# Sixty-six products of zeros in eleven moving-row forms, set between the two products of the first SwiGLU

## The chip, the cores and the metric

The kernel runs on one core of one Trainium2 chip. The metric is device time in microseconds (us), the median over runs of the whole program; lower is better. Profile times are counted from the start of the span, which runs from the first to the last instruction.

## The reference

One layer of a streaming encoder on an input of 1024 tokens by 1024 channels, in float32. The part that matters here is the first of three residual sub-layers:

```python
def swiglu_ffn(x, w_in, w_out):
    gate, up = jnp.split(x @ w_in, 2, axis=-1)
    return (jax.nn.silu(gate) * up) @ w_out

h = h + 0.5 * swiglu_ffn(rmsnorm(h, norm_ffn1[l]), ffn1_w_in[l], ffn1_w_out[l])
# w_in: 1024 x 5632, w_out: 2816 x 1024
# then: one projection to q, k, v, gates and pool; retention; pooling; merge; output product
# then: a second SwiGLU of the same shape, and a last RMSNorm
```

## The kernel before, in words

Every large product is done with one level of Strassen's scheme or more: the operands are cut into blocks (L11 to L22 for the weights, R11 to R22 for the activations), sums of blocks (S1 to S4, T1 to T4) are made on VectorE, and seven products of blocks take the place of eight. Each operand is held as two float32r tiles, a rounded part and the rest, and a product of two operands is three TensorE products (`mm3`, lines 181, 182 and 183): rounded by rounded, rounded by rest, rest by rounded. ScalarE writes the rounded part (line 161, `copy(hi, src)`) and VectorE the rest (line 162, `tt(lo, src, hi, SUB)`). One TensorE product has 128 by 128 weights and mostly 512 moving columns; in the steps made by `common` it has 256. Each has a weight load of its own.

The program is one stream of steps. A step is a pair: `prep`, which issues the loads, the block sums and the splits, and `body`, which issues TensorE's products and the work on their results. `Flow.run` issues the prep of a step four steps (`LOOK`) ahead of its body, and after every body some small items from a queue of follow-up work. A scheduler then orders the instructions of each engine by this order and by when their buffers come free, so an engine may run well ahead of the order of the text where its inputs and buffers are there. Each engine then works through its own list in order; DMAs are nearly all issued by SyncE (SP), also in order.

The buffers are rings. The ones that the change uses are `raw` (4 tiles of 128 by 1024 float32, which receive weights from memory), `c2` (8 tiles of 128 by 512 float32, which hold block sums and half results) and `ps` (6 banks of PSUM, taken with `bank`). The split weights of a step go to a ring of 5 tiles, `wt`.

The first SwiGLU, `ffn1`, runs two generators one after the other. `ffn_in` makes the gate and up halves, 22 groups of 128 channels each, the last two of them as a pair from `pairs_of_both` and `common`; its tiles carry the prefix `a`. Its last steps in TensorE's order are the products into `a_x`, `a_b` and `a_e`. `ffn_out` makes the second product, 11 blocks of the inner dimension, with tiles of the prefix `b`: first the alternating steps `p1` and `p6` for all 11 blocks (`bp1a`, `bp6b` in PSUM), then `p2` and `p7`, and so on. `p1` and `p6` take their weights from `bra` and `bL22a` and block sums `bs` (lines 886 to 888); `bL22a` is a `raw` tile for two blocks at a time, and from block 4 on `bra` is one too. The activations (`br`) are read back from the memory to which `ffn_in` wrote them.

At the start of the kernel, before any weight has arrived, twelve products of bfloat16 zeros (`set<-zero`, line 204) already run on TensorE.

Of the kernel before, what the change touches and what calls it, by code (L numbers as in the profile page):

```python
# [11 lines left out]
F32R = mybir.dt.float32r  # L12
BF16 = mybir.dt.bfloat16
AF = mybir.ActivationFunctionType
ALU = mybir.AluOpType
ADD, SUB, MUL = ALU.add, ALU.subtract, ALU.mult

P = 128
S = 1024
D = 1024  # L20
KT = D // P
H = S // 2  # L22
# [28 lines left out]
N_MV, N_T4, N_RAW, N_WT, N_TL, N_C2 = 28, 9, 4, 5, 4, 8  # L51
# [39 lines left out]
def block_kernel(ctx: ExitStack, tc, x, x_tok, vecs, f1_in, f1_out, w_in, w_v, pool_w, w_ret, w_pool, w_o,  # L91
                 f2_in, f2_out, g_row, rope, decay, consts, out, out_tok):
    nc = tc.nc
    mm = nc.tensor.matmul
# [3 lines left out]
    copy = nc.scalar.copy  # L98
# [4 lines left out]
    sb = ctx.enter_context(tc.tile_pool(name="sb", bufs=1))  # L103
# [16 lines left out]
    def raw(name):  # L120
        return sb.tile([P, S], F32, tag="raw", bufs=N_RAW, name=name)
# [7 lines left out]
    def c2(name):  # L129
        return sb.tile([P, H], F32, tag="c2", bufs=N_C2, name=name)  # L130

    def bank(name):
        return ps.tile([P, H], F32, tag="ps", name=name)

    def sum_bank(name):

        return ps.tile([P, H], F32, tag="sum", bufs=N_SUM, name=name)
# [8 lines left out]
    def spill(name, n, width=S):  # L146
        return [dr.tile([P, width], F32, tag=f"{name}{i}", name=f"{name}{i}") for i in range(n)]

    def half(t, j):
        return t[:, j * H : (j + 1) * H]  # L150
# [49 lines left out]
    for n in range(N_SUM):  # L200
        b = sum_bank(f"set{n}")
# [913 lines left out]
    gates = spill("gt", 2 * KT)  # L1115
    pm, ret = spill("pm", KT), spill("ret", KT)

    def ffn1():
        for n, step in enumerate(ffn_in(first, f1_in, ops1, "a", lead)):
            flow.rate = 1  # L1120
            yield step
        flow.rate = 2
        yield from ffn_out(first, ops1, ops_done["a"], f1_out, x, "b", mix.quarter, end1)

    mix = Next("n2", V_MIX, h1)
# [795 lines left out]
    def second():  # L1921
        for n, step in enumerate(ffn_in(ffn2, f2_in, ops2, "c")):
            flow.rate = 1
            yield step
        flow.rate = 2
    flow.run(chain(ffn1(), projections(), retention(), merge(), second(),
                   ffn_out(ffn2, ops2, ops_done.setdefault("c", set()), f2_out, h2, "d", fin.quarter, fin.end, fin)))
    flow.some(-1)
# [86 lines left out]
```

## Time and profile before

| | before |
|---|---|
| runs, us | 2138.69 and 2139.97, median 2139.33 |
| span of the profiled execution, us | 2137.8 |
| time of the profiled execution | not listed apart; the runs lie 0.9 to 2.2 us above the span |
| TensorE (PE) busy | 2127.8 us, 10798 products |
| weight loads (PEld) busy | 1808.3 us, 10798 loads |
| VectorE (DVE) busy | 1873.2 us, 3352 instructions |
| ScalarE (ACT) busy | 1100.9 us, 2082 instructions |
| GpSimd (POOL) busy | 0.2 us, 4 instructions |
| mean granted TensorE clock | 0.999 |

A product's busy time is longer than its share of the time, since products are pipelined: one with 512 columns is shown as 389 ns, but the next starts before it has ended. What one product costs is therefore read from the number of products in a stretch. In a table by stretches each engine has its busy time and, in brackets, the number of its instructions that touch the stretch.

### The profile page before, as it was taken

To read this page: it belongs to the slowest core of one execution; us is meant where nothing else is said; L and a number is where in the kernel's file an instruction comes from. 1 tells how busy PE (TensorE), PEld (TensorE's weight loads), DVE (VectorE), ACT (ScalarE), POOL (GpSimd) and SP (SyncE) were. 2 spreads that over 40 slices of the span, in tenths; PEclk is the share of its full clock that TensorE was granted. 3 is DMA by queue.
4 is the path that set the end of the run, shared out by engine and by line. 5 is a ranking of instruction groups with operands and counts; after the bars stand their busy time and mean duration, and the time that the engine had idled before them with its cause. 6 is when DMAs were issued, how large, how long until landed. Compare 5 with 4: busy or idle time off the path is not lost.

```text
span 2137.8 us, 30138 instructions
## 1 busy us (share of the span) xinstructions
PE 2127.8 (100%) x10798; PEld 1808.3 (85%) x10798; DVE 1873.2 (88%) x3352; ACT 1100.9 (51%) x2082; POOL 0.2 (0%) x4
## 2 busy tenths in 40 slices
PE   9999999999999999999999999999999999999998
PEld 7888888888888888888888998888888888888887
DVE  8798888997986799999988988899988988899796
ACT  8544444454654534454457753456644544455454
POOL 0000000000000000000000000000000000000000
PEclk9999999999999999999999999999999999999999
DMA  7232323675543333332336666624133232358542
GB/s 251 83 133 75 138 84 129 202 266 187 172 138 98 110 109 119 109 124 104 119 129 223 197 226 236 236 89 163 64 103 119 87 126 85 132 199 276 192 138 99
DMA packets 116391, 313.60 MB, mean 147 GB/s; under 512 B 12817, under 2 KB 17041, under 8 KB 116241
## 3 DMA queue, kind: packets, MB, share of 16 engines
q1 hardware_dynamic: 115664, 310.63, 42.7%
q8 instruction: 84, 1.38, 0.3%
q10 hardware_dynamic: 576, 1.05, 0.1%
q14 instruction: 67, 0.54, 0.1%
HBM read 220.93 MB, written 90.70 MB: 146 GB/s over the span
## 4 chain that ended last, share of the span: by engine, by line
PE 94%; DVE 4%; ACT 1%; DMA 1%; issue 0%; SPq 0%; ACTq 0%; DVEq 0%
PE c_b L181 2%; PE c_b L182 2%; PE c_b L183 2%; PE a_b L181 2%; PE a_b L182 2%; PE a_b L183 2%; PE c_e L182 2%; PE c_e L181 2%; PE c_e L183 2%; PE a_e L182 2%; PE a_e L181 2%; PE a_e L183 2%; PE a_a L181 1%; PE a_a L183 1%; PE a_a L182 1%; PE c_a L181 1%
## 5 line engine op out<-in xcount | busy, mean ns | idle before, releaser
L182 PE MATMUL c_b<-n3T,c_wS 128*128 128x512 f32 x176 | 68.6, 390 | 0.0
L183 PE MATMUL c_b<-n3T,c_wS 128*128 128x512 f32 x176 | 68.5, 389 | 0.0
L181 PE MATMUL c_b<-n3T,c_wS 128*128 128x512 f32 x176 | 68.4, 390 | 0.0
L182 PE MATMUL a_b<-n1T,a_wS 128*128 128x512 f32 x168 | 65.4, 389 | 0.0
L181 PE MATMUL a_b<-n1T,a_wS 128*128 128x512 f32 x168 | 65.4, 389 | 0.0
L183 PE MATMUL a_b<-n1T,a_wS 128*128 128x512 f32 x168 | 65.3, 389 | 0.0
L181 PE MATMUL a_a<-n1R,a_wL 128*128 128x512 f32 x120 | 46.7, 389 | 0.0
L182 PE MATMUL a_a<-n1R,a_wL 128*128 128x512 f32 x120 | 46.7, 389 | 0.0
L183 PE MATMUL a_a<-n1R,a_wL 128*128 128x512 f32 x120 | 46.7, 389 | 0.0
L182 PE MATMUL c_a<-n3R,c_wL 128*128 128x512 f32 x112 | 43.6, 389 | 0.0
L181 PE MATMUL c_a<-n3R,c_wL 128*128 128x512 f32 x112 | 43.6, 389 | 0.0
L183 PE MATMUL c_a<-n3R,c_wL 128*128 128x512 f32 x112 | 43.6, 389 | 0.0
L183 PEld LDWEIGHTS c_b<-n3T,c_wS 128*128 128x128 f32 x176 | 33.0, 188 | 6.9
L182 PEld LDWEIGHTS c_b<-n3T,c_wS 128*128 128x128 f32 x176 | 33.0, 188 | 6.8 <-DVE n3T L162 0.2
L181 PEld LDWEIGHTS c_b<-n3T,c_wS 128*128 128x128 f32 x176 | 33.0, 188 | 6.8 <-ACT n3T L161 0.3
L183 PEld LDWEIGHTS a_b<-n1T,a_wS 128*128 128x128 f32 x168 | 31.5, 188 | 6.6
L181 PEld LDWEIGHTS a_b<-n1T,a_wS 128*128 128x128 f32 x168 | 31.5, 188 | 6.5
L182 PEld LDWEIGHTS a_b<-n1T,a_wS 128*128 128x128 f32 x168 | 31.5, 188 | 6.3
L162 DVE TENSOR_TENSOR a_wS<-a_S,a_wS 128x512 fp32r<-128x512 f32 x45 | 31.0, 690 | 6.7 <-ACT a_wS L161 6.7
L161 ACT CAST c_wS<-c_S 128x512 fp32r<-128x512 f32 x46 | 27.9, 624 | 13.2 <-DVE c_S L455 7.1
L182 PE MATMUL c_e<-n3T,c_wL 128*128 128x512 f32 x88 | 34.5, 393 | 0.0
L181 PE MATMUL c_e<-n3T,c_wS 128*128 128x512 f32 x88 | 34.4, 391 | 0.0
(3385 smaller groups left out, 8156.9 us busy)
## 6 DMA issues: line engine op xcount, KB each, us to landing
c_ra<-in_f_in SPq DMA_DIRECT2D x22, 512.0 KB, 3.8
c_rb<-in_f_in SPq DMA_DIRECT2D x22, 512.0 KB, 3.7
a_ra<-in_f_in SPq DMA_DIRECT2D x21, 512.0 KB, 3.9
a_rb<-in_f_in SPq DMA_DIRECT2D x21, 512.0 KB, 3.9
t<-au SPq DMA_DIRECT2D x11, 512.0 KB, 2.8
b<-ag SPq DMA_DIRECT2D x11, 512.0 KB, 4.3
r<-au SPq DMA_DIRECT2D x11, 512.0 KB, 3.7
bra<-in_f_out SPq DMA_DIRECT2D x11, 512.0 KB, 6.3
```

What stands on the lines that cost most here:

```text
L161: copy(hi, src)
L162: tt(lo, src, hi.bitcast(F32), SUB)
L181: mm(dst, w[0], m[0], start=start, stop=False, skip_group_check=True)
L182: mm(dst, w[0], m[1], start=False, stop=False, skip_group_check=True)
L183: mm(dst, w[1], m[0], start=False, stop=stop, skip_group_check=True)
```

## The change

A new step, made by `forms`, is put between the last step of `ffn_in` and the first of `ffn_out`. Its prep takes two `raw` tiles (`fz`, `fm`) and three `c2` tiles (`fh`, `fy`, `fv`), sets them to zero on VectorE, copies `fz` to `fm` as float32r on ScalarE, does three multiplications by 1 and three copies of 128 by 512 on VectorE, and four subtractions of 128 by 512 on GpSimd, which read `fz` and `fy` and write the second half of `fz`. Its body issues eleven kinds of product, six of each, into one PSUM bank that nobody reads. The weights are 128 columns of `fm` (float32r) or of `fh` (bfloat16); the moving rows are 512 elements of the same tiles, taken in these forms:

| form | rows |
|---|---|
| `m[:, :H]`, `m[:, 8 : H + 8]` | 512 neighbours, from element 0 and from element 8 |
| `h[:, :H]`, `h[:, H:]` | 512 neighbours, bfloat16 |
| `two` | two runs of 256, 512 apart |
| `lines` | 32 runs of 16, 32 apart |
| `pairs_` | every second element |
| `turns` | runs of 16, in turn from the first and the second half of the tile |
| `apart` | single elements, in turn from the first and the second half of the tile |
| `same` | the same 16 elements 32 times |
| `one` | the same element 512 times |

```diff
     gates = spill("gt", 2 * KT)
     pm, ret = spill("pm", KT), spill("ret", KT)
 
+    def forms():
+
+        t = {}
+
+        def prep():
+            z = raw("fz")
+            nc.vector.memset(z, 0.0)
+            t["m"] = sb.tile([P, S], F32R, tag="raw", bufs=N_RAW, name="fm")
+            copy(t["m"], z)
+            t["h"] = sb.tile([P, 2 * H], BF16, tag="c2", bufs=N_C2, name="fh")
+            nc.vector.memset(t["h"], 0.0)
+            y, v = c2("fy"), c2("fv")
+            nc.vector.memset(y, 0.0)
+            for n in range(3):
+                nc.vector.tensor_scalar(v, y, 1.0, None, MUL)
+            for n in range(3):
+                nc.vector.tensor_copy(v.bitcast(F32R), y)
+            for n in range(4):
+                nc.gpsimd.tensor_tensor(half(z, 1), half(z, 0), y, SUB)
+
+        def body():
+            m, h = t["m"], t["h"]
+            w = m[:, S - P :]
+            lines = m.rearrange("p (a b c) -> p a b c", b=2, c=16)[:, :, 0]
+            pairs_ = m.rearrange("p (a b) -> p a b", b=2)[:, :, 0]
+            two = m.rearrange("p (a b c) -> p a b c", a=2, b=2)[:, :, 0]
+            turns = m.rearrange("p (b a c) -> p a b c", b=2, c=16)[:, :16]
+            apart = m.rearrange("p (b a) -> p a b", b=2)[:, :256]
+            same = m[:, :16].unsqueeze(1).to_broadcast([P, 32, 16])
+            one = m[:, :1].to_broadcast([P, H])
+            kinds = [(w, m[:, :H]), (h[:, :P], h[:, :H]), (w, two), (w, lines), (w, pairs_), (w, turns), (w, apart),
+                     (w, same), (w, one), (h[:, :P], h[:, H:]), (w, m[:, 8 : H + 8])]
+            b = bank("forms")
+            for l, r in kinds:
+                for n in range(6):
+                    mm(b, l, r, start=n == 0, stop=n == 5)
+
+        return prep, body
+
     def ffn1():
         for n, step in enumerate(ffn_in(first, f1_in, ops1, "a", lead)):
             flow.rate = 1
             yield step
         flow.rate = 2
+        yield forms()
         yield from ffn_out(first, ops1, ops_done["a"], f1_out, x, "b", mix.quarter, end1)
```

## The prediction

> **What bounds the kernel now.** I read the busy times first, then TensorE's waits, then a table by stretches.
>
> ```profile
> span 2137.8 us, 30138 instructions
> PE 2127.8 (100%) x10798; PEld 1808.3 (85%) x10798; DVE 1873.2 (88%) x3352; ACT 1100.9 (51%) x2082; POOL 0.2 (0%) x4
> PE 94%; DVE 4%; ACT 1%; DMA 1%; issue 0%; SPq 0%; ACTq 0%; DVEq 0%
> ```
> ```profile
> engine line waited for: us in total, times, longest us
> PE set L204 <- DVE zero L199: 1.2, 1, 1.2
> PE a L181 <- ACT n1R L165: 0.8, 2, 0.6
> PE a L182 <- DVE n1R L166: 0.6, 2, 0.3
> PE wo0e L183 <- DVE wo0wS L162: 0.4, 1, 0.4
> PE px L181 <- DVE g3A L1158: 0.4, 1, 0.4
> PE st L182 <- DVE v L162: 0.2, 1, 0.2
> ```
>
> TensorE is busy for all but 10.0 of 2137.8 us and carries 94% of the chain that ended last. Its listed waits are small, and none of them is at the place of the change: those on `set`, `a` and `n1R` are in the kernel's first steps, `px`, `st` and `wo0e` belong to the pooling, retention and merge, after the first SwiGLU. So TensorE is a conveyor: what is put on it makes the kernel longer by its full length, and there is no idle stretch near the place into which it could fall. What remains is to price a product in each form, and to ask whether the preparation delays TensorE or relieves it.
>
> ```profile
> core 0: us, PE busy (x) PEld busy (x) DVE busy (x) ACT busy (x) POOL busy (x), PEclk, DMA share, GB/s
> 408.00:414.00 6.00, 6.00 (x34) 5.22 (x33) 5.93 (x11) 3.90 (x8) 0.00 (x0) 1.00 0.96 300
> 414.00:423.00 9.00, 9.00 (x56) 8.01 (x55) 7.53 (x13) 4.51 (x8) 0.00 (x0) 1.00 0.99 362
> 423.00:440.00 17.00, 17.00 (x76) 14.08 (x75) 17.00 (x28) 6.63 (x12) 0.00 (x0) 1.00 0.52 194
> 430.00:630.00 200.00, 200.00 (x884) 165.58 (x884) 171.06 (x281) 104.68 (x185) 0.00 (x0) 1.00 0.60 199
> ```
> ```profile
> 422.58 0.39 PE L183 MATMUL a_e<-n1T,a_wL 128*128 128x512 f32 x1
> 422.81 0.39 PE L181 MATMUL bp1a<-bp1m,bp1w 128*128 128x512 f32 x1
> ```
>
> The second fence is TensorE's timeline at the seam: the last product of the first half starts at 422.58, the first of the second half at 422.81, with nothing between. The change goes there. The first fence shows TensorE full on both sides of it, and VectorE nearly so: idle for 0.07 us in 408 to 414, 1.47 in 414 to 423 and not at all in 423 to 440.
>
> **The price of one product.** The stretch from 430 to 630 holds only 512-column products of float32 tiles. 884 of them touch it; one that started up to 0.39 us before also counts, so each costs (200 + 0.39) / 884 = 0.2267 us, its weight load hidden (PEld counts 884 too). The bfloat16 price comes from the end of the kernel's opening products:
>
> ```profile
> 5.41 0.38 PE L204 MATMUL set<-zero 128*128 128x512 bf16 x1
> 5.63 0.38 PE L204 MATMUL set<-zero 128*128 128x512 bf16 x1
> ```
>
> These start 0.22 us apart: one spacing only, but it says that bfloat16 rows, of half the bytes, are hardly cheaper. Nine of the eleven kinds are float32r, 54 products of 0.2267 = 12.24 us; two are bfloat16, 12 of 0.22 = 2.64 us. At the plain price the body is 14.88 us.
>
> **The price of the form.** The trace has nearly no moving rows that are not neighbours. The nearest is the scores' product of line 1558, which takes two runs of 128 from the two halves of an operand tile:
>
> ```profile
> 1153.54 0.28 PE L182 MATMUL g2b<-n2R,g2ws 128*128 128x256 f32 x1
> 1153.66 0.28 PE L182 MATMUL s<-q,k 128*128 128x256 f32 x1
> 1153.77 0.28 PE L1558 MATMUL s<-q,k 128*128 128x256 f32 x1
> 1153.89 0.44 PE L181 MATMUL g3e<-n2T,g3wL 128*128 128x512 f32 x1
> ```
>
> It takes 0.12 us to the next start, as its plain neighbours do (0.12 and 0.11): one jump inside a row costs at most the 0.01 us that the view resolves. `two` has one jump, `lines` and `turns` have 31, `same` returns 31 times, `one` never moves, and the row from element 8 only starts elsewhere. For these I take the plain price. Below it they can't go far: bfloat16 rows, with half the bytes to fetch, save only 0.007 each, so even if `same` and `one` saved that, it is 0.1 in all. Upwards the bound is 0.01 per jump, 0.31 for a product of `lines` or `turns`.
>
> `apart` jumps at every element, 511 times, and `pairs_` skips every second one. The lower end is nothing extra. The upper end, 0.01 per jump, is 5.1 us for one product of `apart`, 30.7 for its six. I take twice the plain price for `apart`, one further element's time (0.44 ns) per jump: a jump of that size would be invisible in the row of line 1558, which is the nearest, and a jump at every element leaves no neighbour to share a fetch with. That adds 6 x 0.2267 = 1.36 us. `pairs_` I leave at the plain price; twice would add another 1.36.
>
> The Trainium skill, "Advanced Engine Details and Errata", section "SBUF Cachelines", says that SBUF is read in lines of 16 bytes and that at least two hits on a line are needed for full speed. By it only `apart` would pay (each of its elements leaves the line that the one before it was on) and `pairs_`, with two elements on each line, would not; it gives no amount, and no row here shows such a pattern.
>
> So the body is 14.88 + 1.36 = 16.24 us on TensorE, all of it on the path.
>
> **The preparation.** These rows give its prices:
>
> ```profile
> L199 DVE MEMSET zero<- x1: 272/272/272, 0.9 to 0.9; 128x256 uint32 x1
> L1658 DVE TENSOR_SCALAR o<-o,ir0r x8: 343/347/348, 1207.0 to 1209.2; 128x256 f32<-128x256 f32 x8
> L162 DVE TENSOR_TENSOR a_wS<-a_S,a_wS 128x512 fp32r<-128x512 f32 x45 | 31.0, 690 | 6.7 <-ACT a_wS L161 6.7
> L763 ACT ACTIVATE ag<-ag 128x1024 f32<-128x1024 f32 x22 | 23.4, 1062 | 11.7 <-DVE ag L755 7.3 <-DVE ag L758 4.3
> ```
>
> VectorE: the zeros are 1024, 512 and 512 words, 8 times the 256 words that took 0.272, so at most 2.2 us. The three multiplications of 512 lie between the 0.35 of 256 columns and twice that, the three copies (no row) between the same 0.35 and the 0.69 of a 512-column instruction with two inputs: together 2.1 to 4.2. VectorE gets 4.3 to 6.4 us of new work. ScalarE gets one copy, about 1.06 us, on an engine half idle here (4.51 of 9.00). GpSimd's four subtractions have no row; VectorE's form of the same instruction is 0.69, so at least 2.8 us for four; with GpSimd otherwise empty they cost nothing by themselves. Above, I allow 16 us, the body's length, beyond which they would outlast the cover.
>
> Does this hold TensorE up ahead of the body? What is queued behind the new instructions on VectorE are the last evacuations and the last split of the first half:
>
> ```profile
> 417.28 0.42 DVE L589 TENSOR_TENSOR ag<-a_x,ag 128x256 f32<-128x256 f32 x1
> 417.62 0.68 DVE L162 TENSOR_TENSOR a_wL<-a_rb,a_wL 128x512 fp32r<-128x512 f32 x1
> ```
> ```profile
> 419.38 0.28 PE L181 MATMUL a_x<-n1R22y,a_ws 128*128 128x256 f32 x1
> 420.53 0.39 PE L183 MATMUL a_e<-n1T,a_wL 128*128 128x512 f32 x1
> ```
>
> The product into `a_x` at 419.38 must wait until the addition that ends at 417.70 has read the bank: 1.7 us of slack. The first product with the rest part of `a_wL` starts at 420.53, 2.2 us after its split ends at 418.30. Before them VectorE is not doing only urgent work. It makes block sums for the second half far ahead:
>
> ```profile
> L886 DVE TENSOR_TENSOR bs<-bra,bL22a x11: 686/694/704, 405.0 to 463.0; 128x512 f32<-128x512 f32 x11
> L140 SPq DMA_DIRECT2D bL22a<-in_f_out x11: 327/371/994, 398.1 to 458.3; - x11
> ```
>
> The first of these sums is made at 405.0, for a step `p6` that starts twelve products after 422.81, at 425.5. This run-ahead work gives way to the new work, and the body's 16 us then repay it: VectorE gains 16 us and owes 4.3 to 6.4, plus what GpSimd takes from it. So most of the preparation is hidden. If it fell whole ahead of the two rows above, TensorE would stop for 6.4 - 1.7 = 4.7 us; at best for 0. I take 0.8, about one VectorE instruction that comes at the wrong moment, nearer to 0 because there are some 12 us of VectorE's list between 405.0 and 417.3 in which sums can be exchanged for zeros.
>
> The rings. `fz` and `fm` take two of four `raw` tiles, so `bL22a`, first loaded at 398.1, comes later, and `fm` is held until the body ends, near 439. The next claims of those two tiles are the loads of block 4, first needed by the step eight steps (8 x 12 x 0.2267 = 21.8 us) after the body; SP may stand at one of them until 439, with the later loads queued behind it, and 20 us are left for a landing and a split. The first `bL22a`, moved to some 412 to 418, is needed at 425.5 + 16 = 441. The three `c2` tiles and the bank come after tiles whose readers are done or stand on TensorE itself. I cost the rings at nothing; without the body's cover the late `bL22a` would cost TensorE several us.
>
> **Sum.** 16.24 + 0.8 = 17.0 us. The span becomes 2154.8; the median lies 1.5 above the span, so the time becomes 2156.3. That is 0.8% more, within the 2% (42.8 us, that is 2182.1) that a measurement of this kernel can surely tell from no change.
>
> **Rivals.**
>
> 1. GpSimd holds VectorE up. Both engines read the same tiles, and no row shows GpSimd at work beside VectorE. If each subtraction, at 1.4 us (twice VectorE's 0.69), kept VectorE out for its length, VectorE would lose 5.6 us besides the 4.3 to 6.4, just in 408 to 423, where it has 1.5 us to spare: TensorE stops for up to 5.6 + 6.4 - 1.7 = 10 us, likelier about 5: 2161, at most 2166. For it: VectorE's full rows; against it: the run-ahead work. The Trainium skill, "SBUF — State Buffer", section "Who interferes with whom", speaks for this: a VectorE instruction with two SBUF inputs contends with a GpSimd instruction that reads SBUF, and the later one is blocked until the first is done. No run here shows it yet. Chance 0.17.
>
> 2. Rows apart are dear (the slower side). If a jump costs close to what the view can hide, 9.1 ns, `apart` takes 0.23 + 511 x 0.0091 = 4.9 us a product instead of 0.45: 2156.3 + 6 x 4.45 = 2183, over 2%. It decides from about 9 ns a jump, some twenty times the time of one element. For it: nothing excludes it; against it: the row of line 1558. At 1 to 5 ns a jump it adds 0.5 to 2.6 us to a product: 2158 to 2170. Chance 0.12 for the milder form, 0.03 over 2%.
>
> 3. The body costs less than its count: the 16 us of cover for VectorE take away waits of TensorE later, or the products overlap something. Against it: only 10 us of idle TensorE exist, and most of that in the opening. At most 4 us: 2145 to 2152. Chance 0.08.
>
> 4. The products aren't there in the end (nobody reads their bank), and only the preparation is left: 2139 to 2142. Nothing in the trace speaks for it; the opening products, whose banks nobody reads either, are there in the profile. Chance 0.02.
>
> The forecast itself, 2152 to 2160, has 0.58. The range, 2150 to 2168, takes in rival 1, most of the milder rival 2 and part of rival 3, and leaves out the rest. Faster by over 2% needs 42.8 us that TensorE doesn't lose anywhere: 0.01. Slower by over 2%: 0.03 and 0.01 for a stall that I haven't seen. Within: 0.95.
>
> **What the changed profile would show.** 66 more products (10864) and as many loads; a stretch of some 16 us between the last `a_e` and the first `bp1a` in which only they run, at 0.227 for the float32 kinds, 0.22 for bfloat16, 0.45 for `apart`. TensorE's idle time should grow by less than 1 us. Wrong would be: gaps ahead of the body with VectorE or GpSimd as their releaser (rival 1), other forms over 0.3 or `apart` over 1 us (rival 2), a gap after the body that waits for `bL22a` or `bra` (the rings).

## The result, and the profile after

| | before | after |
|---|---|---|
| runs, us | 2138.69 and 2139.97, median 2139.33 | 2156.92 and 2157.77, median 2157.35 |
| span of the profiled execution, us | 2137.8 | 2154.8 |

The ratio is 1.0085, with a 95% interval of 1.0056 to 1.0115: 18.0 us more, within 2%. Forecast were 2156.3 and a span of 2154.8. The totals fit well; the terms behind them do not, as the profile shows.

First the page's totals and TensorE's list of waits (in total, times, longest):

```profile
span 2154.8 us, 30287 instructions
PE 2145.1 (100%) x10862; PEld 1819.8 (84%) x10864; DVE 1881.4 (87%) x3361; ACT 1102.9 (51%) x2083; POOL 5.8 (0%) x8
```
```profile
PE set L204 <- DVE zero L199: 1.2, 1, 1.2
PE g2b L181 <- ACT g2ws L161: 0.5, 1, 0.5
PE wo0e L183 <- DVE wo0wS L162: 0.4, 1, 0.4
PE a_x L181 <- DVE ag L589: 0.3, 1, 0.3
```

Idle TensorE is 9.7 us against 10.0 before: the whole growth of the span, 17.0 us, is busy time. (Two product records are missing from this trace, so it counts 10862 and not 10864.) One wait is new at the place of the change, that of `a_x` for the addition of line 589, one of the two that the prediction had named. By the starts of the products on both sides TensorE lost 0.49 us there.

TensorE's timeline, the first recorded product of each kind in the order of the code, and the first product of the next step. The columns are start, duration, engine and line:

```profile
422.36 0.39 PE L1153 MATMUL forms<-fm 128*128 128x512 f32 x1
423.95 0.38 PE L1153 MATMUL forms<-fh 128*128 128x512 bf16 x1
424.84 0.58 PE L1153 MATMUL forms<-fm 128*128 128x512 f32 x1
426.42 0.41 PE L1153 MATMUL forms<-fm 128*128 128x512 f32 x1
427.90 0.61 PE L1153 MATMUL forms<-fm 128*128 128x512 f32 x1
430.60 0.42 PE L1153 MATMUL forms<-fm 128*128 128x512 f32 x1
432.06 0.38 PE L1153 MATMUL forms<-fm 128*128 128x512 f32 x1
433.35 0.39 PE L1153 MATMUL forms<-fm 128*128 128x512 f32 x1
434.78 0.38 PE L1153 MATMUL forms<-fm 128*128 128x512 f32 x1
436.09 0.39 PE L1153 MATMUL forms<-fh 128*128 128x512 bf16 x1
438.79 0.40 PE L181 MATMUL bp1a<-bp1m,bp1w 128*128 128x512 f32 x1
```

The body takes 438.79 - 422.36 = 16.43 us; 16.24 was forecast. A kind's price is the difference of two starts, divided by six. The fifth kind, `pairs_`, takes (430.60 - 427.90) / 6 = 0.450 us a product, and the seventh, `apart`, (433.35 - 432.06) / 6 = 0.215. The prediction had it the other way round: 0.2267 and 0.4534. `lines` takes 0.247, `turns` 0.243, `same` 0.238, `one` 0.218.

What the preparation did is in the timeline of VectorE and GpSimd (the lists of `fz` and `fv`: duration minimum, median and maximum in ns, then first and last start):

```profile
L1136 POOL TENSOR_TENSOR fz<-fz,fy x4: 1294/1360/1620, 409.0 to 413.5; 128x512 f32<-128x512 f32 x4
```
```profile
L1132 DVE TENSOR_SCALAR fv<-fy x3: 1402/1402/1515, 410.8 to 413.8; 128x512 f32<-128x512 f32 x3
L1134 DVE CAST fv<-fy x3: 414/420/426, 416.0 to 417.4; 128x512 fp32r<-128x512 f32 x3
```
```profile
408.00:414.00 6.00, 6.00 (x39) 5.38 (x39) 5.69 (x7) 2.01 (x5) 4.76 (x4) 1.00 0.41 128
440.00:460.00 20.00, 20.00 (x90) 16.56 (x89) 17.80 (x29) 9.34 (x16) 0.00 (x0) 1.00 0.85 273
```
The second of these stretches in the kernel before:
```profile
440.00:460.00 20.00, 20.00 (x90) 16.54 (x89) 20.00 (x35) 11.87 (x21) 0.00 (x0) 1.00 0.88 302
```

Each subtraction on GpSimd takes 1.36 us, and beside them the three multiplications on VectorE take 1.4 us each, as long as a subtraction, while the copies of the same size after them take 0.42. The third fence is the table by stretches (columns as in the prediction): between 408 and 414 VectorE gets through 7 instructions where it got through 11 before. Yet by 440 to 460 it has idle time, 2.2 of 20 us, where before it had none: the body's 16 us gave back more than the preparation took.

### The profile page after: what moved, and what is told of

Read it like the earlier page. It is cut to its first block, busy times and chain, and to the rows that moved or that the text cites. A ratio compares the mean times of both kernels' runs of the same rounds, so it can differ in the third digit from the quotient of the medians.

```text
span 2154.8 us, 30287 instructions
## 1 busy us (share of the span) xinstructions
PE 2145.1 (100%) x10862; PEld 1819.8 (84%) x10864; DVE 1881.4 (87%) x3361; ACT 1102.9 (51%) x2083; POOL 5.8 (0%) x8
## 4 chain that ended last, share of the span: by engine, by line
PE 93%; DVE 5%; DMA 1%; issue 1%; ACT 1%; SPq 0%; ACTq 0%; DVEq 0%
PE c_b L181 2%; PE c_b L182 2%; PE c_b L183 2%; PE a_b L181 2%; PE a_b L183 2%; PE a_b L182 2%; PE c_e L182 2%; PE c_e L181 2%; PE c_e L183 2%; PE a_e L181 2%; PE a_e L182 2%; PE a_e L183 2%; PE a_a L181 1%; PE a_a L183 1%; PE a_a L182 1%; PE bp6b L183 1%
```

## Experiments

Ratios are against the kernel before on the same chip, whose median there was 2138.64 to 2138.77 us.

### All products of one kind

```diff
-            kinds = [(w, m[:, :H]), (h[:, :P], h[:, :H]), (w, two), ...
+            kinds = [(w, apart)] * 11      # apart66
+            kinds = [(w, pairs_)] * 11     # step2_66
```

> All 66 products take single elements in turn from two halves of the tile. As the prediction priced it (0.4534 each) the body is 29.9 us and the time 2139.3 + 29.9 + 0.8 = 2170.0; as the trace after shows it (0.216) the body is 14.3 us and the time 2139.3 + 14.3 + 0.5 = 2154.1.

> All 66 products take every second element. As the prediction priced it (0.2267 each) the time is 2139.3 + 15.0 + 0.8 = 2155.1; as the trace after shows it (0.452) the body is 29.8 us and the time 2139.3 + 29.8 + 0.5 = 2169.6. With the run of single elements in turn this is the reverse of the prediction's two choices, whose errors would cancel in the sum.

Measured: `apart66` 2155.21 us (ratio 1.0079, 1.0062 to 1.0096), `step2_66` 2171.34 (1.0150, 1.0135 to 1.0165). The two differ by 16.1 us, 0.244 a product; the prices in the trace after differ by 0.235. In the traces of these two kernels the 66 products take 14.24 us (421.81 to 436.05) and 29.90 us (421.87 to 451.77), that is 0.216 and 0.453 each. So the prediction's two choices were each wrong, in opposite directions, and nearly equal in size. In the whole change, with six products of each, the errors cancelled by luck.

### Which rows are dear

Two kernels with other rows in the step of zeros, eight products of each kind, without the multiplications, copies and subtractions. They are read by the starts of the products alone; each ran once (2159.49 and 2164.39 us). These functions make the rows, and the rest of the edit is left out:

```diff
+            def alt(x, n=2):
+                return x.rearrange("p (b a) -> p a b", b=n)
+            def near(x, n):
+                return x.rearrange("p (c b a) -> p c a b", b=2, a=n)
+            def step(n):
+                return m.rearrange("p (a b) -> p a b", b=n)[:, :, 0]
+            def runs(n):
+                return m.rearrange("p (a b c) -> p a b c", b=2, c=n)[:, :, 0]
+            def swap(n):
+                return m.rearrange("p (b a c) -> p a b c", b=2, c=n)[:, : H // (2 * n)]
```

> The step of zeros with other rows: thirteen kinds, eight products each, no GpSimd and no VectorE work beyond setting the zeros. It is read by the spacing of the products. Theory A, of the trace after: float32 rows come from one stretch of memory at about 9.0 bytes per ns (512 neighbours, 2048 bytes, 0.227 us; every second element, 4096 bytes of stretch, 0.452), and two places far apart supply twice that, so that TensorE's own 0.216 is left. It expects 256 columns of every fourth element 0.45 and 128 columns of every eighth 0.45 (0.23 if a fetch is 16 bytes or less), and 0.216 for the distances 512 and 256; at which smaller distance the gain ends is open. Theory B, of the prediction: every jump costs, so distances 512, 256, 128, 64 all take 0.45, and every fourth or eighth element costs the plain price of its width, 0.113 and about 0.11. Theory C: the 11 ns between 0.227 and 0.216 come from the weights, read from the same tile as the rows; then neighbours with weights from another tile take 0.216.

The first table's timeline, first products: `near(q, 4)` (order 0, 4, 1, 5, 2, 6, 3, 7 in every eight elements), four runs in turn, 256 columns of every fourth element, 128 of every eighth:

```profile
433.98 0.38 PE L1151 MATMUL forms<-fm 128*128 128x512 f32 x1
435.70 0.43 PE L1151 MATMUL forms<-fm 128*128 128x512 f32 x1
439.79 0.39 PE L1151 MATMUL forms<-fm 128*128 128x256 f32 x1
441.64 0.40 PE L1151 MATMUL forms<-fm 128*128 128x128 f32 x2
```

At a distance of 16 bytes a product takes (435.70 - 433.98) / 8 = 0.215 us; the distances 64, 256, 512, 1024 and 2048 bytes took 0.216 too, four runs 0.283. 256 columns of every fourth element take (441.64 - 439.79) / 8 = 0.231, and not 0.45, so what counts is not the stretch of memory spanned; 256 neighbours take half of it, 0.12. 128 columns of every eighth element take 0.11. Neighbours with weights from another tile took 0.227. Theories A, B and C all fell.

> A second table of rows, twelve kinds of eight products. The first table showed 0.216 us for taking single elements in turn from two runs at every distance from 2048 down to 16 bytes, 0.283 for four runs, 0.233 for 256 columns of every fourth element, and weights from elsewhere changed nothing. Theory A (two far places supply twice) has fallen. Theory D: TensorE fetches float32 rows by pairs of addresses that its innermost pattern gives, and a pattern whose innermost step is not 1 is fetched otherwise; by it the order 0, 2, 1, 3 within every four elements (distance 8 bytes) also takes 0.216. Theory E: a fetch unit of 16 bytes must be left; by it that order takes 0.227 or more. Runs of 2, 4, 8 with as many skipped: by stretch of memory they would take 0.45; by the number of jumps they lie between 0.247 (runs of 16, measured) and 0.452 (runs of 1), near 0.35 for runs of 2. Runs of 2, 4, 8 in turn from two halves lie between 0.216 and 0.240 if a run's start costs nothing, above if it does. Each element twice in a row: no theory. Rows from element 2: 0.227.

The second table's timeline, first products: `near(q, 2)` and, in the second line, its last two; then `runs(2)`, `runs(4)`, `runs(8)`, `swap(2)`, `swap(4)`, `swap(8)`, each element twice in a row, `near(q, 8)`:

```profile
422.52 0.39 PE L1158 MATMUL forms<-fm 128*128 128x512 f32 x1
424.11 0.50 PE L1158 MATMUL forms<-fm 128*128 128x512 f32 x2
427.09 0.63 PE L1158 MATMUL forms<-fm 128*128 128x512 f32 x1
430.70 0.41 PE L1158 MATMUL forms<-fm 128*128 128x512 f32 x1
432.58 0.39 PE L1158 MATMUL forms<-fm 128*128 128x512 f32 x1
434.45 0.50 PE L1158 MATMUL forms<-fm 128*128 128x512 f32 x1
437.11 0.42 PE L1158 MATMUL forms<-fm 128*128 128x512 f32 x1
439.12 0.41 PE L1158 MATMUL forms<-fm 128*128 128x512 f32 x1
441.07 0.38 PE L1158 MATMUL forms<-fm 128*128 128x512 f32 x1
442.79 0.38 PE L1158 MATMUL forms<-fm 128*128 128x512 f32 x1
```

The order 0, 2, 1, 3 takes 0.227 (the last starts 1.59 us after the first, seven spacings): the same as neighbours. Theory D fell and E stood: among rows that read each element once, the gain needs a step that leaves the 16 bytes. Runs of two with two skipped take (430.70 - 427.09) / 8 = 0.451, as much as every second element, while runs of four with four skipped take 0.235. These four fit a count of the 16-byte units in which more than one element is read in a row: 128 units in neighbours and in runs of four, 256 in runs of two and in every second element, hence 0.227 and 0.451, that is 1.77 us per thousand units. The units from which single elements are taken cost less: 0.42 ns each in `apart`, 0.91 in every fourth element. Three kinds do not fit: four runs in turn, which leave the 16 bytes at each element too (0.283), runs of two in turn from two halves (0.333), and each element twice in a row (0.215). So the count is a description of some prices and not the mechanism, which stays open. Rows from element 2, the last kind, take 0.233 where 0.227 was expected, and the kernel's own plain products right after them take as long at first; differences of that size between forms are not read here.

### The preparation alone, the products alone

```diff
-            for l, r in kinds:
-                for n in range(6):
-                    mm(b, l, r, start=n == 0, stop=n == 5)
+            return                         # prep_only
```
```diff
-            y, v = c2("fy"), c2("fv")
-            ...
-                nc.gpsimd.tensor_tensor(half(z, 1), half(z, 0), y, SUB)    # body_only: zeros for m and h alone
```

> The step of zeros with its whole preparation and no products. The prediction says that the body's cover repays the preparation: without it TensorE could stop for up to 4.7 us, or 10 with GpSimd's share, so 2139 to 2149; from the trace after, where one wait of 0.49 us ahead of the body is all that the preparation cost, and VectorE had caught up by 457, 2140 to 2144. If the preparation is free even uncovered, 2139.3.

> The step of zeros with all 66 products, but without the three multiplications, the three copies and the four subtractions; only the zeros themselves are made. If the body is the whole cost, the sum of the spacings measured in the trace after, 16.4 us, stands above the kernel before, and nothing else: 2155.7; the difference to the whole change then is the wait of 0.5 us ahead of the body.

> The whole change once more, on the same chip as the kernel with the products alone, for the comparison: 18 us above the kernel before, 0.5 to 2 us above the products alone.

| | us | above the kernel before |
|---|---|---|
| prep_only | 2147.23 (2145.29 to 2149.34) | 8.5; ratio 1.0041, 1.0026 to 1.0056 |
| body_only | 2156.42 (2155.79 to 2156.65) | 17.7; ratio 1.0081, 1.0066 to 1.0096 |
| after_again | 2157.29 (2156.95 to 2159.49) | 18.5; ratio 1.0088, 1.0073 to 1.0103 |

Alone the preparation costs 8.5 us and the products 17.7; together they cost 18.5 and not 26.1. The products' time hides nearly all of the preparation. What is left of it is 0.9 us: the runs of the two kernels do not overlap, but those of `after_again` alone spread by 2.5 us. The wait of `a_x` was there again in `after_again` (0.3) and absent with the products alone. Of the products' 17.7 us the body itself is 16.4; where the other 1.2 are lost is not shown. The preparation alone came out above the 2140 to 2144 expected from the trace after, within the 2139 to 2149 that the prediction's bounds give. Idle TensorE is 15.0 us there (2145.2 less 2130.2 busy), 5.0 more than before. Where the largest part of that arises is in four views of `prep_only`: the waits of TensorE and ScalarE, SP's timeline, SP's waits, and the table by stretches:

```profile
PE bp1a L181 <- ACT bp1w L161: 3.1, 1, 3.1
ACT bp1w L161 <- DMA bra<-in_f_out: 4.8, 1, 4.8
```
```profile
439.06 0.45 SPq L140 DMA_DIRECT2D bra<-in_f_out  x1
```
```profile
SPq L140 <- POOL fz L1136: 3.4, 1, 3.4
```
```profile
445.00:447.00 2.00, 1.85 (x4) 1.50 (x5) 1.99 (x5) 0.56 (x2) 0.00 (x0) 0.50 1.03 380
```

TensorE waits for a split, that for a load of `bra`, and that load was issued only at 439.06, behind SP's own waits; it is the fifth of `bra` after 400, and in the kernel before the fifth goes out at 418.71. The wait of 3.4 us for GpSimd to release `fz` comes before 416; SP's waits from 424 to 439 are all for VectorE, which is busy for 32.6 of the 33 us from 408 to 441. So the delay reaches TensorE through the rings and SP's order, which the prediction had costed at nothing under the body's cover and at "several us" without it. How much of it is the two tiles held and how much VectorE's added work was not tried. The last line shows what the wait brought besides: after 3.5 us without a product the granted clock (third figure from the end) is 0.50, and the trace has products of 512 columns 0.427 us apart until 447.9. The Trainium skill, "TensorE: Matmul & The Clock Gate", part 1 ("The HAM clock gate"), says that an idle window of about 3.4 us halves the clock and as much sustained work restores it; this agrees with the halving, and the slow stretch lasted 2.7 us here.

### Without GpSimd

```diff
-            for n in range(4):
-                nc.gpsimd.tensor_tensor(half(z, 1), half(z, 0), y, SUB)
```

> The step of zeros without GpSimd's four subtractions. In the trace after VectorE's three multiplications took 4.4 us beside them. The rival that GpSimd holds VectorE up says that these fall to about 1.5 us, a_wL's split from 1.25 to 0.69, and the wait of 0.49 us ahead of the body goes: 2156.8 against 2157.3. If the multiplications are slow by themselves, they stay at 4.4.

The list of `fv` in this kernel, and the split of `a_wL`, first in the trace after and then in this kernel:

```profile
L1132 DVE TENSOR_SCALAR fv<-fy x3: 414/422/423, 412.5 to 414.7; 128x512 f32<-128x512 f32 x3
```
```profile
409.59 1.25 DVE L162 TENSOR_TENSOR a_wL<-a_rb,a_wL 128x512 fp32r<-128x512 f32 x1
```
```profile
410.79 0.69 DVE L162 TENSOR_TENSOR a_wL<-a_rb,a_wL 128x512 fp32r<-128x512 f32 x1
```

The multiplications fall from 1402 to 422 ns, so GpSimd had held them up, by about 1 us each. The split, which reads two tiles in SBUF, ran beside the first subtraction in the trace after (409.00 to 410.30) and falls from 1.25 to 0.69 us. The wait of `a_x` is not in TensorE's list. The time, 2155.61 us (2155.30 to 2157.64; ratio 1.0079, 1.0062 to 1.0096), overlaps that of the whole change, and the order of VectorE's list changed too. So the blocking is shown and its price on the path, 0 to some 1.7 us, is not resolved. The Trainium skill, "SBUF — State Buffer", section "Who interferes with whom", counts a multiplication by a constant among the operations that can take the port that VectorE shares with GpSimd; the 1402 ns agree. The rule for two inputs, which the prediction cited, is borne out by the split's 1.25 us.

### Putting the cheap order to use

Rows taken in turn are 11 ns cheaper per product than the kernel's own rows. Four kernels without the step of zeros try this on the real operands. The main lines of the first three edits, the rest left out:

```diff
 # turned_out: operands of the second products, stored in turn in halves, read in turn
+        src = src.rearrange("p (a b) -> p a b", b=2)
+        split(turns(m[:, 0]), turns(m[:, 1]), src)
 # turned_both: SwiGLU rows read in the order 0, 2, 1, 3
+        return x.rearrange("p (c b a) -> p c a b", b=2, a=2)
 # eighths: SwiGLU rows read in the order 0, 4, 1, 5, 2, 6, 3, 7; the evacuation of the second product reads so too
+        return x.rearrange("p (c b a) -> p c a b", b=2, a=4)
```

> The kernel before, without the step of zeros; only the operands of the second products of both SwiGLUs are stored so that reading them in turn from their two halves of 256 gives the old order (the split writes in that order, the product reads in that order). If reading in turn saves 11 ns a product also with real operands, some 1750 products of 512 columns save 19 us: 2120, unless the splits on VectorE and ScalarE become slower by writing in turn; VectorE is full here, so a split of 0.69 us that doubled would undo the gain: 22 steps in each of the two products' first stretches have 1.2 us of VectorE time to spare at most, and the time would be above 2139. If reading in turn only helps products whose rows and weights lie as in the step of zeros, 2139 or more.

2152.97 us (ratio 1.0066, 1.0051 to 1.0081). The products gained: their median spacing is 0.216 against 0.227. The splits lost more. Their groups in the kernel before, then in this one:

```profile
L161 ACT CAST bp6m<-br 128x512 fp32r<-128x512 f32 x11 | 6.8, 618 | 0.0
L162 DVE TENSOR_TENSOR bp6m<-br,bp6m 128x512 fp32r<-128x512 f32 x11 | 7.7, 696 | 0.0
```
```profile
L161 ACT CAST bp6m<-br 128x512 fp32r<-128x512 f32 x11 | 12.7, 1150 | 0.0
L162 DVE TENSOR_TENSOR bp6m<-br,bp6m 128x512 fp32r<-128x512 f32 x11 | 12.7, 1156 | 0.0
```

With writing in turn ScalarE takes 1150 instead of 618 ns and VectorE 1156 instead of 696. Idle TensorE grew from 10.0 to 29.0 us, most of it waits for VectorE.

> The kernel before, without the step of zeros; in both SwiGLUs the products read their moving rows in the order 0, 2, 1, 3 within every four elements. The first product of each thus leaves the hidden values in that order, the second one's reading puts them back, and only the row of norms is stored in that order for the first. No split changes its pattern, except 11 in the second SwiGLU's last steps. If the order takes 0.216 instead of 0.227, the two SwiGLUs' some 5800 products of 512 columns save up to 63 us and those of 256 up to 2 to 3 ns each: 2139 - 60 = about 2080 if VectorE, at 1873 of then 2078 us, keeps up, 2100 if it holds some of it back. If the order takes 0.227, 2139; if it is fetched as slowly as every second element (0.452), some 3400.

2138.81 us (ratio 1.0001, 0.9992 to 1.0011): within four neighbours the order changes nothing, as the second table had shown for zeros.

> The kernel before, without the step of zeros; in both SwiGLUs the products read their moving rows in the order 0, 4, 1, 5, 2, 6, 3, 7 within every eight elements. The second table showed that the order 0, 2, 1, 3 saves nothing (0.227) and that leaving the 16 bytes at every element does (0.216 at a distance of 16 bytes). Three such orders one after the other are the old order, so the first product, the second one and the evacuation of the second's banks apply one each; the splits of the operands stay as they are, apart from 11 at the end. If real operands gain as the zeros did, some 4700 products of 512 columns save 10.9 ns each, 51 us, and 1386 of 256 columns some 3 ns each: 2139 - 55 = 2084. Against it stands that VectorE and ScalarE read banks in that order in 56 evacuations, perhaps 0.45 us longer each (25 us, not all on the path), and that VectorE, nearly full in the first half of the second product, may hold TensorE back: 2084 to 2110. If the gain is not had with real operands, 2139 or more.

2105.36 us, ratio 0.9844 (0.9827 to 0.9860). In the table by stretches 601 products touch 130 us: (130 + 0.38) / 601 = 0.217 us each, with real operands, a short idle time included. Reading a bank in that order costs VectorE nothing: line 986 takes 682 ns, and the same group took 680 in the kernel before. Idle TensorE is 22.6 us, 12.6 more than before; the largest wait is the last of the three views (stretches, groups, waits):

```profile
470.00:600.00 130.00, 129.64 (x601) 113.48 (x601) 113.49 (x187) 69.12 (x124) 0.00 (x0) 1.00 0.56 183
```
```profile
L986 DVE TENSOR_TENSOR bd<-bp5a,brb 128x512 f32<-128x512 f32 x8 | 5.0, 682 | 0.0
```
```profile
PE fin0sum L239 <- DVE n4ssq L276: 5.6, 1, 5.6
```

There 11 splits (`dp4m`) still wrote in the changed order and took VectorE 1118 ns. The last kernel reads in that order in this place too, and takes the order to the Strassen products of the projections, the merge and the output.

> The kernel that reads its rows in the order 0, 4, 1, 5, 2, 6, 3, 7, with the order also in the Strassen products of the projections, the merge and the output product (some 2000 more products of 512 columns), whose evacuations put it back while reading the banks; and the 11 splits at the end write neighbours and read in the changed order, since there the writes in the changed order took 1.1 us instead of 0.69 and left a wait of 5.6 us. If VectorE reads in any such order at no cost, as it did in the first version (0.68 us), 22 us and up to 5 us go: 2105 - 27 = 2078. If reading back by steps of two is slow on VectorE or ScalarE, or VectorE at 89% can't follow, 2085 to 2105.

2086.58 us, ratio 0.9757 (0.9741 to 0.9773): faster than both kernels, and 71 us below the one with the step of zeros. The 11 splits, and the wait that they were held to cause:

```profile
L162 DVE TENSOR_TENSOR dp4m<-dT,dp4m 128x512 fp32r<-128x512 f32 x11 | 7.5, 682 | 0.0
```
```profile
PE fin0sum L245 <- DVE n4ssq L282: 1.5, 1, 1.5
```

Reading in the changed order and writing neighbours costs VectorE nothing (682 ns), so it is the writing that was dear, and the wait fell from 5.6 to 1.5 us. The time is 8.6 us above its forecast, and idle TensorE is 27.8 us. Its waits are many and short, the largest those of `c_x` (2.7 us in six) and `a_x` (1.9 in four) for ScalarE's copies; that these make up the 8.6 us was not tried.

## Why the prediction was right, and where not

- **The conveyor**: right. Idle TensorE stayed the same (10.0 and 9.7 us), and the span grew by the body and 0.6 us.
- **The plain price**: right. Neighbours take 0.227 and bfloat16 0.216; 0.2267 and 0.22 were taken from before.
- **The price of the form**: the failed step. "I take twice the plain price for `apart`" was 1.43 us too high for its six products, and "`pairs_` I leave at the plain price" 1.34 too low. That the two cancel, and that the body came out within 0.2 us, is luck. The prediction's own sign of being wrong, "other forms over 0.3", appeared with the 0.450 of `pairs_`. The row of line 1558 has one jump in 256 elements and could not price either; the upper bounds did hold, and `apart` came out 0.012 us below the lower one. The smaller terms (`lines`, `turns`, `same`, 0.1 each) add the remaining 0.2 or so of the body.
- **The rule weighed against it**: the Trainium skill, "Advanced Engine Details and Errata", "SBUF Cachelines", asks for two hits on a line of 16 bytes. The unit of 16 bytes shows in the tables, but two hits in each are not what float32r rows need: two cost 0.451, four 0.227, and single elements in turn from two places, which leave the unit at every element, 0.215. Leaving it costs something with every fourth element (0.231 for 256 columns, neighbours 0.12) and with four places in turn (0.283). The measurement decides.
- **The preparation**: its size was right. VectorE's list gives 0.91 + 0.48 + 0.48 for the zeros and 0.42 for each of the six others without GpSimd, 4.4 us, against 4.3 to 6.4. 0.8 us was taken for the delay ahead of the body; the trace shows 0.49, at the first of the two rows named.
- **Rival 1** happened in part: GpSimd held VectorE up by about 3 us in the multiplications and 0.6 in the split of `a_wL`, at 1.36 us a subtraction against the assumed 1.4. TensorE lost half a us ahead of the body; the rest was absorbed by work ahead.
- **The rings**: nothing under the cover, as taken, and several us without it, shown by the preparation alone. The late load that TensorE met was `bra`, not `bL22a`.
- **The time around the span**: 1.5 us was the median of two runs less the span of one. The two runs of the change lie 2.1 and 2.2 us above their own spans, 2154.8 and 2155.6. So of the 1.0 us between forecast and measurement 0.6 is this term, and 0.4 comes from the second run's longer span. The runs of the kernel before beside the experiments lie 1.7 to 2.9 us above theirs; no run here explains why.

## What to carry to other kernels

When TensorE is never idle, added products cost their full length, and anything prepared beside them is nearly free up to that length: price the two separately and ask what the cover is worth, which here was 7.6 of 26.1 us. A sum that fits does not show that its terms do: two choices without a row were wrong by 1.4 us each way, and only the price of each kind by itself, in the timeline and in the runs of one kind, could tell. And a probe of zeros can be worth more than its time: the form that looked dearest led to a kernel 2.4% faster.

## What the runs showed of the hardware that was not expected

- A float32r product with 512 moving columns takes 0.227 us with neighbouring elements, 0.216 with single elements in turn from two places 16 to 2048 bytes apart, 0.283 from four places, and 0.451 when only two elements of each 16 bytes are read. Real operands show the first two as zeros do.
- VectorE and ScalarE write 512 float32 in an order that alternates between two halves in 1.15 us instead of 0.69 and 0.62; VectorE reads a bank in the order 0, 4, 1, 5 at no extra cost (682 ns).
- GpSimd's subtraction of 128 by 512 takes 1.36 us, a multiplication by a constant on VectorE beside it 1.40 instead of 0.42, and a split with two inputs in SBUF 1.25 instead of 0.69.
